# A hybrid decoder trunk on one core: the first differential pair's projections ahead of the first latent pair's

## The chip, the cores and the metric

The kernel runs on one core of one Trainium2 chip. The metric is the device time of one execution in microseconds. Five engines of the core work side by side, each through its own queue in order: TensorE (PE, with its weight loads as PEld), VectorE (DVE), ScalarE (ACT), GpSimd (POOL) and SyncE (SP), which here issues DMAs. They wait for each other by semaphores.

## What is computed

The trunk has two layers over 512 tokens with 1024 features. A layer is

```python
h = h + W_out [ MLA(n) | DiffAttn(n) | MoBA(n) ]     # n = RMSNorm(h)
h = h + CrossAttn(RMSNorm(h), RMSNorm(mem))          # mem: 256 rows
h = h + W2 relu(W1 RMSNorm(h))^2
```

and a last RMSNorm follows. The three groups of heads read columns of one input projection of n, and their outputs go through one output projection. MLA has 6 heads with low-rank queries and keys and a rotary part of 32 dimensions, shared by the heads; DiffAttn has 6 heads whose probabilities are the difference of two softmaxes over 32-dimensional queries and keys, with a norm of each head's output; MoBA has 4 heads of 64 dimensions. All are causal. Everything is in f32.

## The kernel before

A product in f32 is made of three matmuls on high and low parts of both factors (`mm3`). So what leaves PSUM is split: ACT casts the high part (L139), and DVE or POOL subtracts it from the value for the low part (L141); where a norm's factor is multiplied in, it is L143 and L144. Weights come by DMA as f32 in blocks, in the order that `planned` gives, and are split the same way (L156 on ACT, L159 on POOL or DVE).

In the mixer the heads go in pairs. m0 to m2 are latent pairs, d0 to d2 differential ones, o0 and o1 MoBA pairs. A pair has 8 units: two heads of four query tiles. The pairs come in the order of `unit_order`, and that is the same in both kernels. For each unit `pipeline` starts it (scores, exponentials L571 and L573, reciprocal L632, multiplication L633), then lets the filler run for a time, then finishes the unit that was started two units earlier (transposes of the probabilities, cast and subtracted at L593 and L596) and, two units after a head's last finish, does the head's tail (`mix`: values times probabilities, L612 and L613).

The filler is a list of generators in the order of `fill_order`: *kv*, *cq* and *tok* (latents, rotary key and the values by token), then the projections of each pair, the memory norm and the cross-attention's keys and values (*cross*). Each part yields its time on PE: `3 * n / 2.4`, which is 640 ns for a part of three matmuls of 512 columns and 320 for 256 columns. d0 and d1 have 16 such parts (8 of the query, 8 of the key), a latent pair has a values part, a keys part and two query parts. The budget of a unit is `fill_time`, by the number of score maps: 2 for differential heads, 1 for the others. The loop is

```python
while self.todo and self.todo[0][2] in self.over and time > 0:
    time -= self.step()
```

Before the first unit of a pair, the filler is drained through that pair's own projections (for d0 and d1, through *tok* at least). Where nothing is left to fill, `self.tick(2)` only lets pending steps go on.

PSUM has three banks of kind `mm` for projections, three of kind `s` for scores and mixes, and two of kind `t` for transposes. In names below, `mm`, `s` and `t` are these banks, `A` the normed input, `B` pairs of high and low parts, `w` split weights, `raw` weights as loaded, `pt` transposed probabilities, `st` stacked queries and keys, `small` values per token. The rotary key goes through DVE (L757 to L761), four transposes on PE, a copy on ACT, a split, and three DMAs on SP; stacks of queries and keys are 12 DMAs per projection on SP.

Of the kernel before, what the change touches and what calls it, by code (L numbers as in the profile page):

```python
# [33 lines left out]
# The tiles of w_in whose outputs come with features on partitions, by first column.  # L34
# [10 lines left out]
# What has one value or more per partition: the gains, by feature, and the frequencies of the rotary embedding.  # L45
# [4 lines left out]
class Filler:  # L50
    """Work that is done in order, a part at a time, between the parts of other work."""
# [5 lines left out]
    def add(self, name, steps, after=None):  # L57
        """Work that may begin when the work `after` is in self.over."""
        self.todo.append((name, steps, after))
# [8 lines left out]
    def run(self, time):  # L68
        """Whether there was any to do."""
        busy = False  # L70
        while self.todo and self.todo[0][2] in self.over and time > 0:
            time -= self.step()
            busy = True
        return busy

    def drain(self, name=None):
        """Does all up to the work of this name."""
        while any(n == name for n, _, _ in self.todo) if name else self.todo:
            assert self.todo[0][2] in self.over
            self.step()  # L80


class Later:
    """Something that comes some time after it is asked for."""
# [4 lines left out]
    def then(self, call):  # L89
        """Makes the call, now or when it is there."""  # L90
        if self.waiting is None:
            call()
        else:
            self.waiting.append(call)
# [7 lines left out]
class Trunk:  # L102
# [13 lines left out]
    # ---------------------------------------------------------------- tiles  # L116
# [16 lines left out]
    # ---------------------------------------------------------------- splits  # L133

    def split(self, hi, lo, x, gain=None, kind=None):
        """x (or x * gain, gain by partition) as hi + lo, each with at most 12 significant bits."""
# [9 lines left out]
    def fetch(self, src):  # L146
        """A [128, n] block of DRAM."""
# [5 lines left out]
    def halve(self, raw, tag="w"):  # L153
        """A block of weights as [128, 2, n] of high and low parts."""
# [7 lines left out]
    def planned(self):  # L162
        """The blocks of weights in the order of their use."""
# [30 lines left out]
    def weights(self, src):  # L194
        """The parts of the next block of the plan, src; the blocks after it are made ready ahead."""
# [10 lines left out]
    def in_order(self, ins, hold=True):  # L206
        """Keeps an instruction of the tensor engine behind the one before it in the program."""
# [12 lines left out]
    def mm3(self, out, lhs, rhs, first, last):  # L220
        """out += lhs^T rhs for lhs, rhs = (high, low)."""
# [5 lines left out]
    def proj_steps(self, src, x, n=S, order=range(KT)):  # L227
        """One tile of 128 output features: [128, n] in PSUM; x(k) gives the pair of input tile k.
        A generator, as all that is called steps: it yields the time on the tensor engine of each part."""
# [16 lines left out]
    def after(self, ticks, call):  # L246
        """Has the call made when as many parts of projections (0.6 us on the tensor engine) are issued."""
        self.hooks.append([ticks, call])
# [14 lines left out]
    def run_all(steps):  # L263
        """What the steps return, after all of them."""
# [6 lines left out]
    # ---------------------------------------------------------------- norms  # L271

    def rsqrt(self, out, x, cols, then=None, ticks=0):
        """out = x ** -0.5 for small [128, cols] tiles: a first value and, some ticks later, a Newton step."""
# [17 lines left out]
    def column_sums(self, sq, ones, ntok, w):  # L292
        """Sums over partitions of sq [128, 128 * ntok], tokens on partitions: [128, ntok * w]."""
# [5 lines left out]
    def row_bcast(self, col, ntok):  # L299
        """A column [128 tokens, ntok] as rows on all partitions: PSUM [128, 128 * ntok]. With a tile  # L300
        [128 tokens, 128 * ntok] for col, its columns become the rows."""
# [14 lines left out]
    def norm(self, sq, ntok, bufs):  # L316
        """The reciprocal rms per token, as column (.col) and rows (.rows), from the sums of squares sq."""
        return self.norm_of(Later(), sq, ntok, bufs)
# [18 lines left out]
    def sum_squares_add(self, x, last, pool=False):  # L337
        """Adds x^2 to the running sum of squares."""
# [12 lines left out]
    def norm_input(self, k, gain, tag="A", squares=True):  # L351
        """The pair of h tile k times its gains, and its squares."""
# [7 lines left out]
    # ---------------------------------------------------------------- constants  # L360

    def setup(self):
        nc, a, const = self.nc, self.a, self.const
        # in the order of need: the first weights, the gains, h
# [31 lines left out]
        # per partition factors of the ALiBi queries: head_dim ** -0.5 / slope  # L396
# [32 lines left out]
    def setup_rotary(self):  # L429
        """The rotary tables."""  # L430
        nc, const = self.nc, self.const
        pc = self.pos_col
        # rotary angles, tokens on partitions: [128, token tile, frequency]
# [39 lines left out]
        def table(name, groups, scale):  # L473
            """[128, tokens] from 16-column groups, one per 16 partitions; None stands for ones."""
# [22 lines left out]
    def setup_distances(self):  # L497
        """Negative distances of positions, with the causal mask."""
# [4 lines left out]
        # positions in two parts, each exact as float32  # L503
# [28 lines left out]
    # ---------------------------------------------------------------- values  # L532

    def evict_values(self, ps):
        """PSUM [128 keys, key tile, 2 heads x 64] to the pair layout [hi | lo | lo | hi] by key tile."""
# [8 lines left out]
    # ---------------------------------------------------------------- softmax attention  # L544

    def stacks(self, p, parts, maps):
        """For the two heads of a pair, the rows of each of the head's maps under one another, as the parts (0 for
        high, 1 for low) say, so that one product takes several of their products."""
# [13 lines left out]
    def scores(self, i, terms, bias, slope):  # L562
        """exp(scores - max) of query tile i, and the sums; the scores are the sum of q^T k over the terms (q, k)."""
# [12 lines left out]
    def transpose_probs(self, i, e, pt):  # L576
        """Blocks of e [128 queries, keys] with keys on partitions, high and low."""
# [7 lines left out]
        # key tile j has the columns KEY_COL[j].. of pt, the first of them for query tile j  # L585
# [15 lines left out]
    def mix(self, v, e, pt, o):  # L601
        """o[64 e:64 e + 64] = values^T probs^T, e the place of the head in its pair."""
# [17 lines left out]
    def head_units(self, maps, bias, slope, v, e, o, mixed, done=None):  # L620
        """The query tiles of a head: (start, finish, tail, time to fill) by tile. maps give the terms of its one or two
        score maps; mixed(sums) gives, for two maps, the factor of the second one's exponentials."""
# [29 lines left out]
    def pipeline(self, units, fill):  # L652
        """The units, each finished some units after it is started, with other work in between."""
# [19 lines left out]
    # ---------------------------------------------------------------- the layer's parts  # L673

    def mixer(self, l):
        """The three groups of heads, two heads at a time: each step's inputs are projected ahead of it."""
# [8 lines left out]
        def latent_steps(srcs, gain, width):  # L685
            """The normed latent of len(srcs) tiles, as pairs, from the projections without the norm of h:
            c r (r^2 mean(c^2) + eps)^-0.5 gain for the reciprocal rms r of the token."""
# [37 lines left out]
        def token_steps():  # L725
            """The values of the first two pairs and the rotary key, tokens on partitions."""
# [37 lines left out]
            def turn(t):  # L764
                """The rotary key, in the rows 64.. of the keys of the two heads of a pair."""
# [19 lines left out]
        def mla_steps(p, got):  # L785
# [9 lines left out]
            # values of two heads, keys on partitions  # L795
# [7 lines left out]
            # keys without position of two heads  # L803
# [57 lines left out]
        def pair_steps(p, got):  # L861
            """Pairs 0 to 2: differential heads; 3 and 4: MoBA heads."""
# [5 lines left out]
            # values: a projection with features on partitions, transposed  # L868
# [15 lines left out]
        def pair_units(p, got):  # L884
# [31 lines left out]
            def done_diff():  # L916
                """The norm of each head's output (which still lacks the factor r1)."""
# [74 lines left out]
    def output(self, w, outs, gain, order=range(KT)):  # L992
        """h += W outs, and what the next norm needs of h."""
# [9 lines left out]
    def memory_norm(self, ticks, step):  # L1003
        """The norm of the memory, the same in all layers but for the gains."""
# [19 lines left out]
    def memory_steps(self, l):  # L1024
        """The memory times its gains, as pairs."""
# [10 lines left out]
    def cross_memory_steps(self, l):  # L1036
        """Keys [features, mem] and values [mem, features] of the memory, as pairs."""
# [15 lines left out]
        # values: memory tokens on partitions, 512 columns of weights at a time  # L1053
# [44 lines left out]
    def cross_units(self, h, qs, outs):  # L1098
        """A head, two query tiles at a time."""
# [24 lines left out]
        def finish(g):  # L1124
# [8 lines left out]
            # columns of pt: memory tile, query  # L1133
# [66 lines left out]
    def finish(self, src, acts):  # L1200
        """The second half of the last product's output tiles and the last norm, for half of the tokens at a time."""
# [6 lines left out]
        def gained(m, cols):  # L1208
            """The tile of h times its gains, in its place."""
# [42 lines left out]
    def run(self):  # L1252
# [4 lines left out]
        # the mixer: the order of the projections and of the pairs of heads, and the time to fill per query tile  # L1257
        self.fill_order = "kv cq tok m0 d0 m1 d1 o0 m2 d2 o1 mem cross"
        self.unit_order = "m0 d0 m1 d1 o0 m2 d2 o1"
        self.fill_time = {1: 1870, 2: 1700}  # L1260
        self.cross_fill_time = 4000
        self.mem_time = 300
        # units from the start of one to its finish, and from there to its tail
        self.skew, self.tail_skew = 2, 2
        # ticks that a chain over several engines waits on the tensor engine for its next part
# [3 lines left out]
        # the splits whose low parts are made by GpSimd  # L1269
        self.pool_kinds = ("mq", "kr", "q", "cq", "lat")  # L1270
        self.vector_full = False
        # blocks of weights that are made ready ahead
# [35 lines left out]
def _layout(inputs):  # L1308
    """The arrays of the launch: the inputs, transposed and cut into the tiles that are loaded."""
# [90 lines left out]
```

## Time and profile before

| | us |
|---|---|
| median of 3 runs | 1570.79 (1569.74 to 1571.38) |
| span of the profiled execution | 1568.8 |
| PE busy in it | 1521.5 (97%) |
| DVE busy | 807.3 (51%) |
| ACT busy | 756.9 (48%) |
| POOL busy | 582.9 (37%) |
| mean granted clock of TensorE | 0.993 |

The span runs from the first to the last instruction of one profiled execution. Busy times are sums over the whole span; they say nothing on where an engine waits. The granted clock is the mean share of full speed that TensorE was given.

### The profile page before, as it was taken

To read this page: it belongs to the slowest core of one execution; us is meant where nothing else is said; L and a number is where in the kernel's file an instruction comes from. 1 tells how busy PE (TensorE), PEld (TensorE's weight loads), DVE (VectorE), ACT (ScalarE), POOL (GpSimd) and SP (SyncE) were. 2 spreads that over 40 slices of the span, in tenths; PEclk is the share of its full clock that TensorE was granted. 3 is DMA by queue.
4 is the path that set the end of the run, shared out by engine and by line. 5 is a ranking of instruction groups with operands and counts; after the bars stand their busy time and mean duration, and the time that the engine had idled before them with its cause. 6 is when DMAs were issued, how large, how long until landed. Compare 5 with 4: busy or idle time off the path is not lost.

```text
span 1568.8 us, 21961 instructions
## 1 busy us (share of the span) xinstructions
PE 1521.5 (97%) x7496; PEld 1270.1 (81%) x7496; DVE 807.3 (51%) x1890; ACT 756.9 (48%) x1620; POOL 582.9 (37%) x469
## 2 busy tenths in 40 slices
PE   7799999999999999999998999999999999999997
PEld 6678797888888888888887878878888888888887
DVE  7688898536333323232336898874363432323333
ACT  5566677535444324242446666764354442423332
POOL 5645365442322222222456445634514222222231
PEclk9999999999999999999999999999999999999999
DMA  4444454231233333333324434423313333333331
GB/s 139 124 109 113 110 145 121 74 95 54 78 91 101 94 94 101 94 98 98 94 77 117 137 91 128 126 80 102 96 34 94 94 100 96 95 100 94 95 114 54
DMA packets 88847, 154.98 MB, mean 99 GB/s; under 512 B 11808, under 2 KB 16800, under 8 KB 88736
## 3 DMA queue, kind: packets, MB, share of 16 engines
q1 hardware_dynamic: 88448, 153.53, 32.9%
q8 instruction: 60, 0.98, 0.3%
q14 instruction: 51, 0.42, 0.1%
q10 hardware_dynamic: 288, 0.05, 0.0%
HBM read 136.24 MB, written 2.10 MB: 88 GB/s over the span
## 4 chain that ended last, share of the span: by engine, by line
PE 82%; DVE 10%; ACT 2%; issue 2%; POOL 1%; DMA 1%; SPq 1%; POOLq 0%; DVEq 0%; ACTq 0%
PE mm L215 72%; PE s L215 7%; PE t L218 3%; DVE tmp L571 2%; DVE B L141 1%; ACT tmp L573 1%; DVE pt L596 1%; DVE tmp L636 1%; POOL w L159 1%; PE t L215 1%; DVE tmp L633 1%; SPq L557 1%; DVE small L911 1%; ACT B L139 0%; DMA st<-B 0%
## 5 line engine op out<-in xcount | busy, mean ns | idle before, releaser
L159 POOL TENSOR_TENSOR w<-raw,w 128x512 fp32r<-128x512 f32 (+2 forms) x328 | 419.1, 1282 | 767.9 <-ACT w L156 729.2
L215 PE MATMUL mm<-A,w 128*128 128x512 f32 (+1 forms) x3072 | 688.3, 380 | 10.8 <-ACT A L143 5.7
L215 PEld LDWEIGHTS mm<-A,w 128*128 128x128 f32 x3072 | 551.1, 189 | 119.5 <-DVE A L144 6.0
L156 ACT CAST w<-raw 128x512 fp32r<-128x512 f32 (+1 forms) x500 | 305.6, 612 | 591.3 <-PE mm L215 509.5
L215 PE MATMUL mm<-B,w 128*128 128x512 f32 x2298 | 535.2, 393 | 4.0 <-DVE B L144 2.2
L215 PEld LDWEIGHTS mm<-B,w 128*128 128x128 f32 x2298 | 430.3, 188 | 100.5 <-DVE tmp L817 2.9
L990 DVE TENSOR_TENSOR h<-mm,h 128x512 f32<-128x512 f32 x92 | 63.6, 691 | 312.4 <-PE mm L215 312.4
L1166 DVE SCALAR_TENSOR_TENSOR tmp<-mm,rows 128x512 f32<-128x512 f32 x64 | 44.3, 692 | 172.5 <-PE mm L215 166.4
L573 ACT ACTIVATE tmp<-tmp,small 128x384 f32<-128x384 f32 (+3 forms) x176 | 99.0, 563 | 67.8 <-DVE small L571 62.2
L159 DVE TENSOR_TENSOR w<-raw,w 128x512 fp32r<-128x512 f32 x172 | 121.5, 706 | 4.9 <-ACT w L156 3.8
L141 DVE TENSOR_TENSOR B<-tmp,B 128x512 fp32r<-128x512 f32 (+1 forms) x106 | 77.6, 732 | 46.7 <-ACT B L139 46.0
L139 ACT CAST B<-tmp 128x512 fp32r<-128x512 f32 (+2 forms) x152 | 90.0, 596 | 16.3 <-DVE tmp L715 4.3
L218 PE MATMUL t<-ident,tmp 128*128 128x128 f32 (+1 forms) x444 | 74.4, 275 | 9.6 <-DVE tmp L761 4.6
L141 POOL TENSOR_TENSOR B<-tmp,B 128x512 fp32r<-128x512 f32 (+1 forms) x46 | 62.6, 1368 | 44.8 <-ACT B L139 39.6
L348 POOL TENSOR_TENSOR tmp<-tmp,tmp 128x512 f32<-128x512 f32 (+1 forms) x37 | 46.6, 1259 | 79.4 <-ACT tmp L345 79.1
L218 PEld LDWEIGHTS t<-ident,tmp 128*128 128x128 f32 (+1 forms) x444 | 54.4, 141 | 24.5 <-issue 6.5
L215 PE MATMUL s<-B,B 128*128 128x256 f32 (+5 forms) x368 | 71.9, 318 | 0.3 <-DVE small L571 0.2
L596 DVE TENSOR_TENSOR pt<-t,pt 128x256 fp32r<-128x256 f32 (+1 forms) x192 | 66.8, 369 | 9.4 <-ACT pt L593 8.8
L215 PE MATMUL s<-pt,B 128*128 128x512 f32 (+3 forms) x352 | 71.0, 345 | 0.0
L593 ACT CAST pt<-t 128x256 fp32r<-128x256 f32 (+1 forms) x192 | 57.9, 333 | 21.4 <-PE t L218 20.4
L215 PE MATMUL mm<-w,A 128*128 128x512 f32 (+1 forms) x288 | 65.9, 369 | 1.5 <-DVE B L144 1.5
L215 PEld LDWEIGHTS s<-pt,B 128*128 128x128 f32 x352 | 58.1, 188 | 6.2
(159 smaller groups left out, 1138.0 us busy)
## 6 DMA issues: line engine op xcount, KB each, us to landing
raw<-w SPq DMA_DIRECT2D x256, 256.0 KB, 2.7
raw<-w_in SPq DMA_DIRECT2D x64, 256.0 KB, 3.0
st<-B SPq DMA_DIRECT2D x144, 64.0 KB, 2.0
raw<-w_ck SPq DMA_DIRECT2D x32, 256.0 KB, 3.0
raw<-w_cv SPq DMA_DIRECT2D x32, 256.0 KB, 2.7
raw<-w_out SPq DMA_DIRECT2D x32, 256.0 KB, 2.9
raw<-w_cq SPq DMA_DIRECT2D x32, 256.0 KB, 2.8
raw<-w_co SPq DMA_DIRECT2D x32, 256.0 KB, 2.6
```

Source lines behind the costliest of these rows:

```text
L139: nc.scalar.copy(hi, x)
L141: eng.tensor_tensor(lo, x, hi.bitcast(F32), ALU.subtract)
L156: self.nc.scalar.copy(w[:, 0, :], raw)
L159: eng.tensor_tensor(w[:, 1, :], raw, w[:, 0, :].bitcast(F32), ALU.subtract)
L215: self.in_order(self.nc.tensor.matmul(out, lhs, rhs, start=start, stop=stop), hold)
L218: self.in_order(self.nc.tensor.transpose(out, x, self.ident))
L348: eng.tensor_tensor(s[:, :n], s[:, :n], self.sq[:, :n], ALU.add)
L573: nc.scalar.activation(t[:, :n], t[:, :n], AF.Exp, bias=st[:, 0:1], scale=-1.0, accum_out=st[:, 1:2])
L593: nc.scalar.copy(hi, src)
L596: nc.vector.tensor_tensor(lo, src, hi.bitcast(F32), ALU.subtract)
L990: nc.vector.tensor_tensor(self.h[m], ps, self.h[m], ALU.add)
L1166: nc.vector.scalar_tensor_tensor(t, ps, 0.0, self.hnorm.rows, ALU.max, ALU.mult)
```

## The change

Two lines are changed. The first puts `d0` ahead of `m0` in the order of the filler; the order of the pairs' units stays. `planned` reads the same list, so the weights of d0 are also loaded ahead of those of m0. The second takes 160 ns from the filler's budget of each unit.

```diff
-        self.fill_order = "kv cq tok m0 d0 m1 d1 o0 m2 d2 o1 mem cross"
+        self.fill_order = "kv cq tok d0 m0 m1 d1 o0 m2 d2 o1 mem cross"
         self.unit_order = "m0 d0 m1 d1 o0 m2 d2 o1"
-        self.fill_time = {1: 1870, 2: 1700}
+        self.fill_time = {1: 1710, 2: 1540}
```

On PE, after the values by token in layer 0, this stood before: m0's values, its keys, a query of two parts with the turn of the rotary key (`t<-ident,tmp`) in it, and then d0's query.

```order
L215 MATMUL mm_709<-w_632,B_574 128x128 x12
L215 MATMUL mm_725<-B_574,w_632 128x512 x3
L215 MATMUL mm_733<-B_623,w_602 128x512 x3
L215 MATMUL mm_733<-B_627,w_602 128x512 x3
L218 MATMUL t_683<-ident,tmp_654 64x128 x4
L215 MATMUL mm_745<-B_623,w_602 128x512 x3
L215 MATMUL mm_745<-B_627,w_602 128x512 x3
L215 MATMUL mm_773<-A_123,w_701 128x512 x3
```

In the kernel after, d0's query comes first, with the turn of the rotary key ahead of its last part; its key (mm_758, not shown) follows, and then m0 and the first parts of m1:

```order
L215 MATMUL mm_683<-A_141,w_632 128x512 x3
L218 MATMUL t_695<-ident,tmp_654 64x128 x4
L215 MATMUL mm_683<-A_144,w_632 128x512 x3
...
L215 MATMUL mm_827<-w_778,B_574 128x128 x12
L215 MATMUL mm_843<-B_574,w_778 128x512 x3
L215 MATMUL mm_851<-B_623,w_761 128x512 x3
L215 MATMUL mm_851<-B_627,w_761 128x512 x3
L215 MATMUL mm_863<-B_623,w_761 128x512 x3
L215 MATMUL mm_863<-B_627,w_761 128x512 x3
L215 MATMUL mm_896<-w_824,B_574 128x128 x12
L215 MATMUL mm_914<-B_574,w_824 128x512 x3
L215 MATMUL mm_933<-B_623,w_819 128x512 x3
```

So the two projections of d0 have moved ahead of m0, and m1's values, keys and first query now stand right behind m0's. On ACT, the evictions of the two latent pairs stand in this order after (64x512 are the keys of one head, mm_843 of m0 and mm_914 of m1; L540 the values):

```order
L139 CAST B_702<-mm_843 64x512
L156 CAST w_893<-raw_891 128x512
L139 CAST B_705<-mm_843 64x512
L139 CAST B_800<-tmp_798 128x512
L139 CAST B_707<-mm_914 64x512
L139 CAST B_709<-mm_914 64x512
L540 CAST B_840<-mm_827 128x4x2x64
L139 CAST B_860<-tmp_858 128x512
```

The casts of m1's keys stand ahead of the cast of m0's values and of m0's first query. At the end of the mixer of layer 0, the last head's units on PE had cross values (mm_3314, mm_3315) between them before:

```order
L215 MATMUL s_3492<-st_2355,st_2247 128x128
L215 MATMUL s_3492<-B_2352,B_2244 128x128
L215 MATMUL mm_3314<-w_3438,A_2491 128x512 x3
L215 MATMUL mm_3315<-w_3438,A_2491 128x512 x3
L218 MATMUL t_3519<-ident,tmp_3418 128x128 x3
L215 MATMUL s_3527<-st_2355,st_2247 128x256
L215 MATMUL s_3527<-B_2352,B_2244 128x256
```

After, the same place holds scores and transposes, and w_out's products (mm_3649) with the heads that are done:

```order
L215 MATMUL s_3428<-st_2246,st_2128 128x128
L215 MATMUL s_3428<-B_2243,B_2125 128x128
L218 MATMUL t_3438<-ident,tmp_3342 128x128 x3
L215 MATMUL s_3446<-st_2246,st_2128 128x256
L215 MATMUL s_3446<-B_2243,B_2125 128x256
L215 MATMUL mm_3649<-B_1903,w_3362 128x512 x3
L215 MATMUL mm_3649<-B_1380,w_3362 128x512 x3
L215 MATMUL mm_3649<-B_2658,w_3395 128x512 x2
```

The cross values have all moved ahead of these units.

## Rows read from the trace of the kernel before

**Rows 1.** The head of the page: span, and busy time of each engine.

```profile
span 1568.8 us, 21961 instructions
...
PE 1521.5 (97%) x7496; PEld 1270.1 (81%) x7496; DVE 807.3 (51%) x1890; ACT 756.9 (48%) x1620; POOL 582.9 (37%) x469
```

**Rows 2.** Windows at the mixer's starts: busy times, clock, DMA share, GB/s.

```profile
45.00:50.00 5.00, 2.94 (x14) 2.94 (x15) 2.51 (x9) 0.20 (x1) 1.50 (x2) 0.57 0.54 170
60.00:65.00 5.00, 2.73 (x14) 1.79 (x13) 3.99 (x7) 1.79 (x4) 2.35 (x2) 1.00 0.27 82
830.00:835.00 5.00, 3.97 (x12) 2.79 (x13) 2.52 (x6) 2.38 (x4) 1.27 (x1) 0.66 0.25 84
```

**Rows 3.** PE's timeline, layer 0: start, duration, work, [idle before <-releaser].

```profile
47.06 1.87 PE L215 MATMUL t<-ones,tmp 128*128 128x2 f32 x8 [4.97 <-DVE tmp L697]
...
56.28 1.45 PE L215 MATMUL mm<-w,B 128*128 128x128 f32 x12
58.85 2.36 PE L215 MATMUL mm<-B,w 128*128 128x512 f32 x9 [1.11 <-DVE B L144]
63.48 0.63 PE L218 MATMUL t<-ident,tmp 128*64 128x128 f32 x4 [2.27 <-DVE tmp L761]
64.08 1.66 PE L215 MATMUL mm<-B,w 128*128 128x512 f32 x6
66.85 3.91 PE L215 MATMUL mm<-A,w 128*128 128x512 f32 x16 [1.11 <-DVE B L141]
70.59 0.85 PE L215 MATMUL s<-B,B 128*128 128x128 f32 x6
...
87.44 1.66 PE L215 MATMUL mm<-B,w 128*128 128x512 f32 x6 [0.90 <-DVE tmp L817]
```

**Rows 4.** PE's timeline, the same place in layer 1.

```profile
826.16 2.33 PE L215 MATMUL mm<-B,w 128*128 128x512 f32 x9 [1.11 <-DVE B L144]
830.79 1.06 PE L218 MATMUL t<-ident,tmp 128*64 128x128 f32 x4 [2.30 <-DVE tmp L761]
831.50 2.85 PE L215 MATMUL mm<-B,w 128*128 128x512 f32 x6
834.59 3.91 PE L215 MATMUL mm<-A,w 128*128 128x512 f32 x16 [0.23 <-DVE B L141]
...
855.13 1.65 PE L215 MATMUL mm<-B,w 128*128 128x512 f32 x6 [0.85 <-DVE tmp L817]
```

**Rows 5.** DVE's timeline in layer 0: m0's key, and the rotary key's last step.

```profile
62.35 0.67 DVE L141 TENSOR_TENSOR B<-mm,B 64x512 fp32r<-64x512 f32 x1
...
63.20 0.23 DVE L761 COPY tmp<-tmp 128x128 f32<-128x128 f32 x1
```

**Rows 6.** Window over o1 in layer 0: PE, PEld, DVE, ACT, POOL, then as above.

```profile
254.70:285.80 31.10, 31.09 (x159) 24.50 (x158) 23.57 (x72) 19.30 (x53) 12.64 (x10) 1.00 0.27 85
```

**Rows 7.** Groups by line and form there: busy us, mean ns | idle before.

```profile
L215 PE MATMUL mm<-w,A 128*128 128x512 f32 x43 | 11.5, 406 | 0.0
...
L596 DVE TENSOR_TENSOR pt<-t,pt 128x256 fp32r<-128x256 f32 x12 | 4.7, 416 | 0.9 <-ACT pt L593 0.8
L593 ACT CAST pt<-t 128x256 fp32r<-128x256 f32 x12 | 4.1, 373 | 1.5 <-PE t L218 1.4
...
L613 DVE TENSOR_TENSOR tmp<-s,tmp 64x512 f32<-64x512 f32 x3 | 2.1, 685 | 0.8 <-ACT tmp L612 0.8
...
L633 POOL TENSOR_SCALAR tmp<-tmp,small 128x256 f32<-128x256 f32 x2 | 1.9, 926 | 5.7 <-DVE small L632 5.7
...
L277 POOL TENSOR_TENSOR small<-small,mhalf 128x8 f32<-128x8 f32 x1 | 1.7, 1668 | 4.3 <-DVE small L927 4.3
...
L633 DVE TENSOR_SCALAR tmp<-tmp,small 128x384 f32<-128x384 f32 x2 | 1.6, 790 | 0.0
...
L573 ACT ACTIVATE tmp<-tmp,small 128x384 f32<-128x384 f32 x2 | 1.2, 619 | 0.3 <-DVE small L571 0.3
```

**Rows 8.** PE's timeline behind o1: the unbroken products of the output projection.

```profile
285.82 7.66 PE L215 MATMUL mm<-B,w 128*128 128x512 f32 x31
```

## The prediction

> **What bounds the kernel now.** I read the page first: the span is 1568.8 us and PE is busy in 97% of it, DVE in 51%, ACT in 48%, POOL in 37% [rows 1]. So the work of PE sets the time, no other engine is near its limit over the whole, and what a reordering can win or lose is PE's idle time (some 47 us in all) and stretches of low clock. I then went along PE's own timeline through the places that the change touches, because the row of a matmul group shows in brackets how long PE stood idle ahead of it and who let it go.
>
> At the start of the mixer of layer 0 there are five such waits [rows 3]. The 4.97 us ahead of the latent queries' sums (47.06) stand before the change's place and stay. Then, in m0: 1.11 for a normed latent, 2.27 for the rotary key (DVE L761), 1.11 for a free bank, and 0.90 for a bank again at 87.44 in m1. The last four make 5.39. In layer 1 the same waits are 1.11, 2.30, 0.23 and 0.85, together 4.49 [rows 4]. There the clock falls too: the window at 830 has a granted clock of 0.66, where its twin in layer 0 at 60 has 1.00 [rows 2]. It shows in the durations: four transposes take 1.06 instead of 0.63 and six query matmuls 2.85 instead of 1.66 [rows 3, 4], so it costs 0.4 + 1.2 = 1.6, and layer 1's start loses 6.1.
>
> At the end of the mixer I took one window from the first scores of the last pair, o1, to the first of the unbroken w_out products: 31.10 us, in which PE is busy for 31.09 [rows 6]. DVE is busy for 23.57 there, 76%, ACT for 19.30. So DVE is much denser in this stretch than over the kernel, and PE still never waits, because the filler's 43 cross-value products [rows 7] stand between the score and probability steps.
>
> **What the change does.** The budgets come first, since they look like half of it. A filler step is taken while the rest is above zero. Parts of 640 against 1870 give three parts (1920); against 1710, three; against 1700 and 1540, three as well. Where a part is 320 (the cross keys) six parts make 1920 under each of the budgets that meet such parts. So nearly every query tile takes the same filler as before: the filler is *not* shortened by what has gone ahead. I cost this edit at nothing in the middle, ± 2 us.
>
> The reorder then takes the 16 parts of d0's query and key out of the filler and puts them ahead of m0, and nothing replaces them. I counted by the program: before, cross parts last through the fifth unit of o1 (3, 3, 3, 3, 2); after, they end with the last unit of d2 (2 parts), and the eight units of o1 have none, in each layer. The order of PE agrees: of the 42 cross matmuls that stand between o1's scores in before, none is left in after, while the w_out matmuls of finished heads that stand ahead of the last mix go from 28 to 30.
>
> **Start of layer 0.** PE comes to m0's place at 56.28 [rows 3]. In after it runs seven parts of d0's query first, at which take (70.59 - 66.85)/16 x 3 = 0.70 each: 4.9, to 61.2. This covers the 1.11 for the normed latent. The rotary key is not ready then: it ended at 63.43, and of what stood ahead of it on DVE only m0's key subtraction (0.67) has gone [rows 5]. So PE waits until some 62.8: 1.65. After that come d0's remaining parts and then m0's values, key and first query, with everything ready. The new waits are for PSUM banks, since m0, m1 and the projections share three: m0's second query waits for the first one's multiplication (0.7), and m1's first query for m1's key bank. That bank is given back when both heads' halves have been cast on ACT and subtracted on DVE, 0.67 each on DVE [rows 5]; a cast is about as long, the two run in turn, 2.65 together. First scores wait another 0.15. Sum: 1.65 + 0.7 + 2.65 + 0.15 = 5.15, against 5.39: a gain of 0.2. In layer 1 it is 5.15 against 6.1: a gain of 0.9, if the clock stays up. At best the bank waits are hidden by other work and only the two rotary waits stay: (5.39 - 1.65) + (6.1 - 1.65) = 8.2 gained. At worst the clock falls at the new bank wait in both layers, 1.6 each [rows 2, 4]: 1.1 - 3.2 = 2.1 lost. I take the middle of the argument, 1.1 gained. Of the DMAs moved with it (two blocks of weights per d0 tile, the twelve copies of the stacks ahead of the three copies of the rotary key on SP) I cost nothing: the DMA share is 0.27 in the window at 60 [rows 2], and no PE wait in [rows 3, 4] is for a weight block.
>
> What the row shows of the clock: after the idle 4.97 it is 0.57, after 1.11 + 2.30 in layer 1 it is 0.66, after 1.11 + 2.27 in layer 0 it is 1.00 [rows 2 to 4]. So waits of this size drop it some of the time. The Trainium skill, "TensorE: Matmul & The Clock Gate", section "HAM oscillation — how this bites in real kernels", says that a loop with little TensorE work between waits falls back to the half clock again and again. By it the unfilled o1 would be paid twice, wait and half clock; by the rows it is paid once unless a wait of over 2 us stands there. That is the second rival below.
>
> **End of each layer.** PE's work in the stretch falls from 31.1 by 42 matmuls and rises by two. A matmul of 512 columns in an unbroken run takes 7.66/31 = 0.247 [rows 8]: 31.1 - 10.4 + 0.5 = 21.2. The 10.4 are the ones done at the start, so they are no gain by themselves; what counts is how much longer than 21.2 the stretch is. DVE keeps all that it did but some 1.4 us of evictions and splits that go with the cross products: 22.2. I laid the queues of PE, DVE, ACT and POOL of after beside each other with the mean durations of the forms, those that the sum names standing in [rows 7], and found PE waiting here:
> - third unit's scores, for the bank that the mix of d2 holds until L613 is done: 0.7 (0.685);
> - transposes behind POOL's multiplication L633 (0.926): 0.65 in two waits;
> - the 384-column unit's transposes, behind the exponentials (0.62) and the multiplication (0.79): 1.2;
> - the broadcast of d2's norm, behind the power on POOL (1.67) and what it waits for: 2.5;
> - the last transposes, cast (0.37 per 256 columns) and subtracted (0.42) before the last mix: 1.35.
>
> Together 6.4, and the stretch would be 27.6 with DVE 80% busy. Were DVE to fill 85% of it, it would be 22.2/0.85 = 26.1 and the loss 4.9. The lower bound is DVE without a pause, 22.2 - 21.2 = 1.0; the upper, with some of the stretch at the low clock, 6.4 + half of the 4.3 that a fallen clock costs below, 8.5. I take 6, near the walk, since a chain of dependent steps rarely closes up: 12 over the two layers.
>
> **The sum.** 1568.8 - 1.1 + 12 = 1579.7 for a profiled span. The median of the runs of before, 1570.8, is 2.0 above its profiled span, so the forecast is 1581.5 us.
>
> **The rivals.**
> - *The clock falls in the unfilled end.* The 2.5 us for d2's norm and the waits around it are of the size that dropped it at 830. Some 6 us of PE work then take 2.85/1.66 = 1.7 times as long: 4.3 per layer more, 1590. Against it: PE stays over 70% busy in my walk. By the Trainium skill's page on the clock this is the rule; before's rows show it once in two. Chance 0.13 (all above 1586).
> - *The unfilled units close up.* DVE paces the end closely (loss 1 to 2 per layer) and the start gives what I worked out: 1568.8 + 2 to 4 - 1.1 + 2.0, about 1572, no change. For it: two head units overlap, and PE has w_out products of finished heads to put between. Chance 0.14.
> - *Faster, because the bank waits are hidden.* The start gains its upper bound of 8.2, PE going on with other units while a bank is cleared, and DVE, the only pacer left, runs the end dense: 1.0 each. 1568.8 - 8.2 + 2.0 + 2.0 = 1564.6. It decides from the point at which the end costs under half of what the start gains less 3.1. Against it: the order of PE in after has nothing else between the key and the query of m1. Chance 0.11.
> - *The change doesn't do what it says*: a filler that really is shortened would spread to the end and cost nothing there. It is ruled out by the arithmetic of 640, so it is part of the forecast.
>
> **Chances.** Slower as forecast, 1574 to 1586: 0.62; above 1586: 0.13. Within 0.2% (3.1 us, about what can be told from no change): 0.14. Faster: 0.11. The range, 1569 to 1588, leaves out the faster cases and the outer part of the clock's.
>
> **What would show it.** In the profile after: PE's wait for L761 at about 61 shrunk to 1.6 us; a new wait of over 2 us for m1's bank; no cross product after the last d2 unit; and in o1's 28 us some 6 us of idle PE with releasers on DVE, ACT and POOL. Wrong would be an o1 as dense as before, a filler still running in it, or a start that is shorter by over 4 us.

## The result, and the profile after

The changed kernel takes 1595.16 us (median of 4 runs, 1593.69 to 1596.39) against 1570.26 in the same comparison: 1.0155 times as long, 95% interval 1.0143 to 1.0167. It is slower, as forecast, but by 24.9 us where 10.7 were forecast, and it lies outside the range.

The head of the page of the kernel after:

```profile
span 1592.3 us, 21956 instructions
...
PE 1533.3 (96%) x7496; PEld 1277.6 (80%) x7496; DVE 803.7 (50%) x1890; ACT 759.4 (48%) x1620; POOL 578.0 (36%) x469
```

Against [rows 1] the span is 23.5 longer, with the same 7496 matmuls. PE's idle time went from 47.3 to 59.0, 11.7 more. PE's busy time went from 1521.5 to 1533.3, 11.8 more for the same work: that half is clock. The mean granted clock fell from 0.993 to 0.986, and 0.014 x 1592.3 - 0.007 x 1568.8 = 11.3, the time that the low clock takes after less that before, agrees.

To see where, I cut each layer's mixer into three stages: the start, from the end of *tok* to m0's first scores; the middle, from there to o1's first scores; and the end, from there to 12 us behind the first sum into h (L990 on DVE). Outside of these stages the two kernels differ by about 1 us. Windows of the kernel before, layer 0 and then layer 1 (length, then PE, PEld, DVE, ACT and POOL busy, granted clock, DMA share, GB/s):

```profile
56.28:70.59 14.31, 9.82 (x49) 7.45 (x48) 9.70 (x22) 9.64 (x24) 10.10 (x9) 1.00 0.43 112
70.59:256.12 185.53, 177.66 (x1013) 150.55 (x1011) 159.91 (x485) 129.85 (x355) 96.12 (x75) 1.00 0.44 123
256.12:301.90 45.78, 45.77 (x219) 35.98 (x219) 31.06 (x81) 27.46 (x64) 18.64 (x16) 1.00 0.28 87
823.59:838.34 14.75, 11.10 (x49) 8.43 (x48) 8.51 (x21) 9.11 (x23) 9.78 (x9) 0.88 0.36 94
838.34:1021.56 183.22, 176.46 (x1007) 149.90 (x1005) 157.02 (x479) 128.76 (x353) 94.72 (x74) 1.00 0.44 122
1021.56:1067.30 45.74, 45.74 (x219) 35.92 (x219) 31.01 (x81) 27.45 (x64) 18.55 (x16) 1.00 0.27 87
```

And of the kernel after:

```profile
56.00:82.58 26.58, 21.52 (x102) 17.24 (x101) 13.70 (x28) 14.08 (x32) 15.03 (x13) 0.94 0.50 127
82.58:270.02 187.44, 178.19 (x1002) 150.25 (x1000) 154.59 (x477) 129.83 (x352) 96.32 (x77) 0.99 0.44 120
270.02:314.80 44.78, 40.72 (x180) 31.12 (x180) 30.72 (x84) 24.53 (x60) 11.14 (x10) 0.92 0.18 54
836.13:861.85 25.72, 20.66 (x102) 16.62 (x101) 11.81 (x26) 12.83 (x30) 13.39 (x13) 0.98 0.44 109
861.85:1046.88 185.03, 178.11 (x995) 151.00 (x994) 152.81 (x472) 129.34 (x351) 96.69 (x76) 0.98 0.44 122
1046.88:1091.20 44.32, 40.24 (x180) 30.88 (x180) 30.75 (x84) 24.45 (x60) 11.17 (x10) 0.92 0.18 54
```

Length less PE's busy time is idle time. Length times one less the clock is roughly what the low clock costs; it counts the idle part of a slow stretch too. Idle, both layers together: start 8.1 before and 10.1 after, middle 14.6 and 16.2, end 0.0 and 8.1; that is 11.6 more. (Of the middle's 14.6 before, 1.75 are the waits for m1's query at [rows 3, 4], which lie in the start after.) Clock: before, only the 1.8 of layer 1's start; after, 3.6 + 3.6 in the two ends, and some 7 in starts and middles, which the two decimals of a long window give only roughly. Short windows of the kernel after show them best, four of layer 0 and five of layer 1 (0.50 is the lower of the clock's two levels; values between 0.50 and 1.00 are means over a window that has both):

```profile
80.00:82.50 2.50, 2.50 (x6) 2.00 (x7) 0.46 (x1) 1.15 (x3) 2.28 (x2) 0.50 0.44 105
97.50:100.00 2.50, 2.50 (x8) 1.96 (x7) 1.71 (x6) 1.77 (x6) 2.50 (x3) 0.53 0.54 166
295.00:297.50 2.50, 2.50 (x9) 2.10 (x9) 1.18 (x3) 0.31 (x1) 0.00 (x0) 0.50 0.00 0
297.50:300.00 2.50, 2.50 (x7) 1.92 (x8) 1.13 (x2) 1.20 (x2) 0.00 (x0) 0.50 0.00 0
860.00:862.50 2.50, 2.50 (x10) 2.14 (x10) 0.58 (x1) 1.27 (x3) 2.16 (x2) 0.70 0.44 104
862.50:865.00 2.50, 2.50 (x10) 2.13 (x10) 2.15 (x9) 1.10 (x4) 0.35 (x1) 0.62 0.40 95
985.00:987.50 2.50, 2.50 (x14) 2.50 (x14) 1.34 (x5) 0.84 (x3) 2.05 (x2) 0.54 0.66 204
1070.00:1072.50 2.50, 2.04 (x9) 1.64 (x9) 1.13 (x2) 0.59 (x3) 0.00 (x0) 0.50 0.02 7
1072.50:1075.00 2.50, 2.50 (x8) 1.96 (x9) 1.35 (x3) 0.58 (x2) 0.00 (x0) 0.50 0.00 0
```

PE's timeline of the kernel after shows what stands ahead of them, at the start of layer 0, at its end, and in the middle of layer 1:

```profile
62.40 0.60 PE L218 MATMUL t<-ident,tmp 128*64 128x128 f32 x4 [1.46 <-DVE tmp L761]
...
73.36 1.67 PE L215 MATMUL mm<-B,w 128*128 128x512 f32 x6 [0.78 <-DVE tmp L817]
...
79.89 2.90 PE L215 MATMUL mm<-B,w 128*128 128x512 f32 x6 [2.82 <-DVE B L141]
...
94.02 0.40 PE L218 MATMUL t<-ident,rcol 128*128 128x128 f32 x2 [0.63 <-DVE rcol L283]
95.82 0.55 PE L218 MATMUL t<-ident,tmp 128*128 128x128 f32 x3 [1.39 <-DVE pt L596]
...
290.53 0.52 PE L218 MATMUL t<-ident,tmp 128*128 128x128 f32 x3 [1.07 <-DVE tmp L633]
293.04 1.06 PE L218 MATMUL t<-ident,tmp 128*128 128x128 f32 x8 [1.99 <-DVE tmp L932]
294.57 2.92 PE L215 MATMUL s<-pt,B 128*128 128x512 f32 x8 [0.46 <-ACT pt L593]
297.28 3.29 PE L215 MATMUL mm<-B,w 128*128 128x512 f32 x7
...
975.22 0.50 PE L215 MATMUL mm<-A,w 128*128 128x256 f32 x2 [0.79 <-DVE A L144]
...
983.10 1.18 PE L215 MATMUL t<-halves,tmp 128*128 128x2 f32 x8 [0.91 <-ACT tmp L920]
```

The wait of 2.82 for m1's key bank is there, and the six matmuls behind it take 2.90 in place of 1.66 [rows 3]; in layer 1 the wait is 2.82 as well. At the end of layer 0, after 1.07 and 1.99 of idle time, the last mix takes 2.92 (1.46 in the earlier units) and seven w_out products 3.29, 0.47 each in place of 0.247 [rows 8].

### The profile page after: what moved, and what is told of

The parts are those of the page before. It is cut to its first block, busy times and chain, and to the rows that moved or that the text cites. A ratio compares the mean times of both kernels' runs of the same rounds, so it can differ in the third digit from the quotient of the medians.

```text
span 1592.3 us, 21956 instructions
## 1 busy us (share of the span) xinstructions
PE 1533.3 (96%) x7496; PEld 1277.6 (80%) x7496; DVE 803.7 (50%) x1890; ACT 759.4 (48%) x1620; POOL 578.0 (36%) x469
## 4 chain that ended last, share of the span: by engine, by line
PE 80%; DVE 10%; ACT 3%; issue 2%; POOL 1%; DMA 1%; SPq 1%; POOLq 0%; ACTq 0%; DVEq 0%
PE mm L215 71%; PE s L215 7%; PE t L218 2%; DVE tmp L571 2%; ACT tmp L573 2%; DVE tmp L636 1%; DVE pt L596 1%; DVE small L911 1%; DVE B L141 1%; POOL w L159 1%; PE t L215 1%; ACT w L156 1%; DVE tmp L613 1%; DMA raw<-w_in 1%; ACT B L139 0%
## 5 line engine op out<-in xcount | busy, mean ns | idle before, releaser
L215 PE MATMUL mm<-A,w 128*128 128x512 f32 (+1 forms) x3072 | 691.4, 381 | 11.8 <-DVE A L144 5.9
L156 ACT CAST w<-raw 128x512 fp32r<-128x512 f32 (+1 forms) x500 | 305.1, 612 | 595.4 <-PE mm L215 514.0
L990 DVE TENSOR_TENSOR h<-mm,h 128x512 f32<-128x512 f32 x92 | 63.6, 692 | 309.0 <-PE mm L215 309.0
L141 DVE TENSOR_TENSOR B<-tmp,B 128x512 fp32r<-128x512 f32 (+1 forms) x106 | 72.5, 690 | 47.4 <-ACT B L139 47.0
L596 DVE TENSOR_TENSOR pt<-t,pt 128x256 fp32r<-128x256 f32 (+1 forms) x192 | 67.0, 370 | 11.9 <-ACT pt L593 11.6
```

The source lines that it names most:

```text
L141: eng.tensor_tensor(lo, x, hi.bitcast(F32), ALU.subtract)
L156: self.nc.scalar.copy(w[:, 0, :], raw)
L215: self.in_order(self.nc.tensor.matmul(out, lhs, rhs, start=start, stop=stop), hold)
L596: nc.vector.tensor_tensor(lo, src, hi.bitcast(F32), ALU.subtract)
L990: nc.vector.tensor_tensor(self.h[m], ps, self.h[m], ALU.add)
```

## The experiments

All times are medians with the ratio to the kernel before, run beside it, and its 95% interval. Each kernel is the one after but for the edit shown, unless the text says otherwise.

**The budgets.** The order of the kernel after with the old budgets, 1870 and 1700, puts the same instructions in the same order on all five engines as the kernel after does, so in this order the budgets change nothing: the 24.9 us are what the order costs, under either pair of budgets. The other way round, the old order with the new budgets:

```diff
-        self.fill_time = {1: 1870, 2: 1700}
+        self.fill_time = {1: 1710, 2: 1540}
```

> The order of the kernel before with the budgets of the kernel after, 1710 and 1540. Theory (the parts are 640 and three are taken under either budget; only parts of 320 at 1540 become five in place of six): no change, 1569 to 1574. Rival (a smaller budget does shorten the filler): over 1578, or under 1567.

Measured: 1574.56 us, 1.0026 (1.0017 to 1.0035). Here the units with two score maps meet the cross keys' parts of 320 and take five of them, where they took six, and the end has 2.3 us of idle PE per layer; how the one makes the other was not followed. So in the old order the budgets cost 4 us, a little over the expectation and under the rival's 1578.

**Filler that lasts to the end.** The overdraft of one unit is taken from the next one's budget, so that 1710 and 1540 hold on average:

```diff
...
+        time -= self.debt
...
         while self.todo and self.todo[0][2] in self.over and time > 0:
             time -= self.step()
+        self.debt = max(0, -time) if busy else 0
...
```

> The changed order is kept and the filler carries what it ran over its budget into the next unit, so that 1710 and 1540 hold on average (2 or 3 parts of 640 per unit in place of always 3), and filler lasts through the last unit of o1. Theory (the unfilled o1 costs most of the 25 us: waits of 5.6 and a low clock of 3.8 per layer): o1 has no idle PE and the clock stays up, 19 us back, about 1576. Rival (the loss is made at the start, by the banks of m0 and m1, and by what follows from it): the end gives back little and units with two parts wait more, 1588 to 1600.

Measured: 1585.39 us, 1.0092 (1.0077 to 1.0107). Windows of the middle and the end of layer 0:

```profile
82.49:255.54 173.05, 162.65 (x930) 137.06 (x929) 149.19 (x476) 122.56 (x340) 84.31 (x67) 0.99 0.42 115
255.54:308.30 52.76, 51.22 (x244) 40.74 (x244) 31.73 (x84) 31.09 (x72) 23.09 (x18) 1.00 0.33 97
```

The end is as the theory has it: 1.54 us of idle time in place of 4.06, and a clock of 1.00 in place of 0.92. But the middle has 10.4 us of idle time (9.25 in the kernel after), and 10 us came back, not the 19 of the theory: the time lies between the theory and its rival. The 19 was also too high from the start: the two ends together hold 2 x (4.06 + 3.6) = 15.3. What the carrying costs by itself was measured on the old order and budgets:

> The order and the budgets of the kernel before, with the overdraft carried, so that 1870 and 1700 hold on average and some units take two parts. It tells what the carrying costs by itself. Theory (what was left over in the run with the changed order and the carried budget, 14 us, comes from the order's start, 2 to 3 per layer, and from thin units, 3 to 4 per layer): 1575 to 1580. Rival (the carrying is free, and all 14 us are the order's): 1569 to 1573.

Measured: 1575.93 us, 1.0037 (1.0023 to 1.0051), as the theory said; its end has the same 1.55 us of idle time. If the two costs add, then of the 14 us that the carried version stays above the kernel before, some 6 are the price of thinner units and the rest belongs to the order; that they add was not tested, and the budgets of the two runs differ.

**m1 away from m0.** d1 also goes ahead of m1:

```diff
-        self.fill_order = "kv cq tok d0 m0 m1 d1 o0 m2 d2 o1 mem cross"
+        self.fill_order = "kv cq tok d0 m0 d1 m1 o0 m2 d2 o1 mem cross"
```

> d1 also goes ahead of m1 in the filler's order, so that m1's values, keys and queries are no longer built right behind m0's. Theory: the wait of 2.82 for the bank of m1's keys and the low clock behind it (1.2 to 1.5) go in both layers, 8 us in all, about 1587; the unfilled end stays as it is. Rival (DVE and ACT at the start are the limit, and the wait only moves to the first scores): 1593 to 1597.

Measured: 1604.93 us, 1.0213 (1.0198 to 1.0228): slower than the kernel after by 10, above the theory and its rival. PE's timeline, layer 0:

```profile
91.67 0.79 PE L215 MATMUL s<-B,B 128*128 128x384 f32 x3 [2.48 <-DVE small L571]
...
109.79 0.45 PE L215 MATMUL s<-st,st 96*128 96x384 f32 x1 [1.20 <-DVE small L571]
111.37 0.49 PE L215 MATMUL s<-st,st 96*128 96x512 f32 x1 [1.14 <-DVE small L571]
112.73 0.51 PE L215 MATMUL s<-st,st 96*128 96x512 f32 x1 [0.86 <-DVE small L571]
115.09 1.22 PE L215 MATMUL mm<-A,w 128*128 128x512 f32 x2 [1.86 <-ACT w L156]
```

The start has indeed 2.24 us of idle time in place of 5.06, and a clock of 1.00. But d1's parts now fill the gap ahead of m0's scores, and the scores of m0 and d0 then wait for L571, DVE's step on the scores ahead of them, and a projection behind them for a split of weights (L156). That the parts which went to the start are what is missing there fits the order, but was not tested by itself. The middle of layer 0 has 14.54 us of idle time and a clock of 0.96. My expectation treated filler as if it were made anew at the start. The two edits, d1 ahead of m1 and the carried overdraft, together:

> d1 ahead of m1, and the carried budget. Theory: the two gains add, 1595 - 19 - 8 = 1568, just under the kernel before. Rival for the sum (the shorter filler gives less cover to the longer score chains of the middle): 1573 to 1580.

Measured: 1595.79 us, 1.0155 (1.0138 to 1.0172), above the theory and its rival. Carrying gives back 9 us here as well; the d1 edit's loss of 10 stays.

**Spare matmuls in the end.** In units without filler, matmuls that nothing reads:

```diff
...
             if not fill.run((u or units[-1])[3]):
                 self.tick(2)
+                if self.outs is not None and (ps is None or u is None and started):
+                    x = self.outs[0][:, 0, :]
+                    n = 1 if ps is None else 6
+                    ps = self.psum("mm") if ps is None else ps
+                    for i in range(n):
+                        self.mm(ps, x[:, :P], x, True, True)
...
```

> The kernel after, with 13 spare matmuls of 512 columns per layer whose result nothing reads: one in o1 and six ahead of each of the last two rounds of transposes, where PE is idle for 1.07 and 1.99 us. Theory (the clock falls there because of the idle time, at 3.8 us per layer, and the time is otherwise free): 7 us faster than the kernel after, about 1588. Rival (the low clock is no cost of these waits, or comes anyway): the 13 matmuls add up to 3.2 us per layer, 1595 to 1602.

Measured: 1595.24 us, 1.0152 (1.0136 to 1.0167), as long as the kernel after. The windows of the end, both layers:

```profile
271.11:315.20 44.09, 41.16 (x193) 31.00 (x193) 29.44 (x84) 24.85 (x60) 11.29 (x10) 1.00 0.18 55
1048.53:1092.50 43.97, 41.01 (x193) 30.90 (x193) 29.33 (x84) 24.75 (x60) 11.17 (x10) 1.00 0.18 55
```

The clock stays at 1.00 in both, so its fall there is a result of the idle time, as the theory has it; the time is the rival's. The 13 matmuls are 3.2 us of work and took only 1.1 us of idle time away, since the transposes queue behind them, and so does the last mix. With the clock's gain the two ends are 0.7 and 0.35 us shorter than in the kernel after, which is less than its runs differ by, and the total shows nothing of it. With seven:

> The kernel after with 7 spare matmuls per layer in place of the 13 of the earlier run: one in o1, three ahead of each of the last two rounds of transposes. With 13 the clock stayed at 1.00 in the end of both layers, which gave back 3.6 us per layer, but the time was the same, since they are 3.2 us of work and took only 1.1 us of idle time away. Theory (the low clock is worth 3.6 per layer, and each spare matmul not covered by a wait costs its 0.25): if 7 keep the clock up, 3 to 5 us faster than the kernel after, 1590 to 1592. Rival (it takes all of the idle time to be filled): the clock falls as in the kernel after, 1594 to 1599.

Measured: 1597.45 us, 1.0168 (1.0151 to 1.0185). The clock falls in the end of both layers, for half as long (0.50 at 295 to 297.5, back at 0.93 in the next window), and the wait of 1.99 for L932 (L938 in this kernel) is as long as in the kernel after. So neither amount of spare work paid for itself here, and what pays in the runs above is work that has to be done anyway.

**Less of d0 ahead of m0.** Only d0's query, with the budgets of the kernel before:

```diff
-        self.fill_order = "kv cq tok d0 m0 m1 d1 o0 m2 d2 o1 mem cross"
+        self.fill_order = "kv cq tok d0q m0 d0k m1 d1 o0 m2 d2 o1 mem cross"
...
+        steps["d0q"] = lambda: qk_steps(3, got["d0"], "q", 0, ((0, 0, 1), 2))
+        steps["d0k"] = lambda: qk_steps(4, got["d0"], "k", None, ((0, 1, 0), 2))
...
```

> Only the query of d0 (8 parts) goes ahead of m0, its key stays between m0 and m1; budgets of the kernel before. Filler then lasts through the second unit of o1. Theory (the key's 8 parts keep m1 away from m0, so the wait of 2.82 and the low clock behind it are gone; of the end, part comes back): start 2.2 us idle per layer in place of 5.1, o1 loses 2 to 5 us per layer, in all 1572 to 1580. Rival (the end is lost as a whole as soon as o1's last units are bare, the 9 us per layer of the kernel after): 1586 to 1590.

Measured: 1576.19 us, 1.0041 (1.0027 to 1.0054). The three windows of layer 0:

```profile
54.92:74.13 19.21, 16.64 (x83) 13.44 (x81) 10.39 (x23) 11.48 (x27) 13.73 (x12) 1.00 0.51 132
74.13:262.00 187.87, 178.03 (x1008) 150.47 (x1006) 156.47 (x482) 129.78 (x354) 95.26 (x76) 0.99 0.44 123
262.00:305.60 43.60, 40.82 (x195) 31.33 (x195) 32.54 (x84) 25.82 (x63) 13.10 (x11) 1.00 0.23 66
```

There is no wait for m1's bank, 2.57 us idle at the start, 2.78 at the end, and no low clock in either. So three quarters of the loss went with 8 of the 16 parts, as the theory said. With the overdraft carried:

> The same, with the overdraft of the budget carried, 1870 and 1700: filler lasts into the seventh unit of o1. Theory: the start's gain is kept and the end costs 1 to 2 us per layer, 1566 to 1572. Rival (units with two parts in place of three cost idle time in the middle, as in the run with the changed order and the carried budget, 2.4 us per layer and the clock): 1573 to 1580.

Measured: 1579.84 us, 1.0068 (1.0046 to 1.0089), the rival's time: the thinner units bring nothing, and the end still has 3.28 us of idle time in layer 0, where the theory had 1 to 2. And with only five parts ahead, on the budgets of the kernel before:

```diff
...
+        gen = pair_steps(0, got["d0"])
+        steps["d0a"] = lambda: (next(gen) for i in range(5))
+        steps["d0b"] = lambda: gen
...
-        self.fill_order = "kv cq tok d0 m0 m1 d1 o0 m2 d2 o1 mem cross"
+        self.fill_order = "kv cq tok d0a m0 d0b m1 d1 o0 m2 d2 o1 mem cross"
...
```

> Only the first five parts of d0's query (3.5 us, about the 3.4 us that PE waits there in the kernel before) go ahead of m0; the rest of d0 stays between m0 and m1; budgets of the kernel before. Theory (each part moved to the start is taken from the end; the first five fill idle time, the other three and the key do not): start 2 to 3 us idle per layer, the end 1 to 2 in place of 2.8, in all 1568 to 1574, level with the kernel before or just under. Rival (m0's queries now wait for the bank that the unfinished query of d0 holds): 1575 to 1582.

Measured: 1586.66 us, 1.0102 (1.0087 to 1.0117), above the theory and its rival. The windows of the start and the middle of layer 0:

```profile
57.02:72.72 15.70, 12.96 (x57) 10.19 (x56) 8.85 (x21) 9.43 (x23) 8.61 (x8) 0.89 0.47 118
72.72:266.93 194.21, 182.41 (x1022) 153.57 (x1021) 161.79 (x485) 131.95 (x359) 98.57 (x78) 0.99 0.42 118
```

The wait for the rotary key is 2.53 here, the clock falls behind it, and the middle has 11.8 us of idle time. The rival's wait for a bank is not it: at m0's queries PE waits 0.17. The longest waits in the middle are 2.36 for the norm of a differential pair (L932) and 1.35 for a split of weights (L156); why they come was not tried. No version of this change that ran beats the kernel before.

## Why the prediction was right in its sign and wrong in its size

**Start.** The waits came as worked out: 1.46 for the rotary key (1.65; the prediction's own 62.8 - 61.2 is 1.6), 0.78 for the second query (0.7), 2.82 for m1's key bank (2.65), 5.06 per layer in all (5.15). The 0.15 ahead of the first scores did not come. What failed is the step "if the clock stays up". It fell behind the bank wait in both layers, for 1.6 in layer 0 and 1.7 in layer 1 (0.75 in the window at 860 and 0.95 in the next), while I took it as a bound only. Instead of a gain of 1.1 the start lost some 2. That the bank wait is what lowers it is supported by the run with only the query ahead: no such wait, and a clock of 1.00 at the start of both layers.

**Middle.** "At nothing, ± 2 us": idle time rose by 3.3 net of the waits that moved to the start, and the clock fell in each layer once more, at 97.5 and at 985, some 1.7 each. Together 6 to 7, the largest miss of the three. The step that failed is "nearly every query tile takes the same filler as before", taken as a reason for no cost. The budgets were not it (same order of instructions), nor were the weights that moved: no wait of PE in the two middles is for a weight block. The units of the middle did keep their parts, but other parts stand in them, and the step looked only at how many. Which part was missing at these two places, and whether that is the whole cause, stays open.

**End.** The count of the filler was right: nothing stands in o1 but w_out. I forecast a stretch of 27.6 from o1's first scores to the unbroken w_out products, with 6.4 of waits; it was 27.3, with 4.1 (0.53, 1.07, 1.99, 0.46). The waits for L932 (2.5 in the walk), L633 (1.2) and the last cast (1.35) came where the walk of the queues put them; the 0.7 for the bank of d2's mix and the 0.65 behind POOL did not, and the 0.53, for L636, was not in the walk. That the length agrees is luck: 2.3 less of waits, and 2 more of PE's busy time (23.2 against 21.2), in which the low clock begins. What was mis-sized is the clock term: I took the end at 6 per layer without it, and it is 4.1 of idle time and 3.6 of clock, and the clock goes on into the w_out products behind the stretch that I had walked. At 7.7 the end lies within the bounds that the prediction gave it, 1.0 to 8.5.

**The rivals.** The failed choice is the one between the forecast and the first rival, "the clock falls in the unfilled end", which I gave 0.13 and priced at 4.3 per layer. It happened in both layers at 3.6, and the same thing at the start and in the middle, so that the rival's 1590 is 5 short as well. By the sum: the forecast of 10.9 is 12.5 of idle time and -1.6 of clock; measured were +11.6 of idle time and some +12 of clock. So the clock is the term that failed. That the idle time agrees is luck in part, since 3.9 too much for the ends (8.1 against 12) stands against 3.3 in the middle that was put at nothing. (By its own terms, 1579.7 + 2.0, the prediction's sum is 1581.7 and not 1581.5, which changes nothing.) The rule of the Trainium skill that I had weighed ("TensorE: Matmul & The Clock Gate", section "HAM oscillation — how this bites in real kernels") agrees with this trace: the clock fell behind 2.82 of waiting and behind 1.07 + 1.99, in both layers. The case of that section is waits for DMAs; the waits here are for other engines. The faster rivals are out: the bank wait was not hidden, and DVE did not run dense in the end (30.72 of 44.78).

**Range.** Its upper end, 1588, held one of the clock's places and not three. At all three PE stood idle shortly before, so the chances of the three hang together, and they should have been taken together. The sign was not luck: the end cost more than the start could give, as the prediction had it.

## What to carry to other kernels

Filler moved to an early gap is taken from a later one, so price both ends, and price each new wait twice: the idle time, and the clock that may fall behind it. Check that a budget's change crosses a whole part before it is counted at all. In a tally, PE's busy time for an unchanged number of matmuls is the row that tells clock from waiting.

## What the runs showed of the hardware

The clock's fall is not told by the length of one wait. Behind 2.82 it fell in both layers of the kernel after (0.50 at 80, 0.70 and 0.62 in the two windows at 860). Behind 1.07 + 1.99 it fell to 0.50, and 13 spare matmuls about these waits kept it at 1.00. A wait of 2.27 left it at 1.00 in layer 0 of the kernel before and one of 2.30 was followed by 0.66 in layer 1 [rows 2 to 4]; the waits of 1.46 for the rotary key in the kernel after left it at 1.00 in both layers. In layer 1 of the kernel after it fell to 0.54 at 985 behind waits of 0.79 (L144) and 0.91 (L920), eight microseconds apart. In layer 0 the same two places have waits of 0.84 and 0.16, and the clock stayed at 1.00; in the run with 13 spare matmuls, which stand later than this place, they are 0.80 and 0.89 in layer 0, and there the clock fell as well.
